# A two-level product scheme on one core: gated factors and modulation steps given out by an account of VectorE's work, weight sums moved from GpSimd to VectorE, raw weights fetched one pair ahead

## The chip, the cores and the metric

One core of one Trainium2 chip runs the whole program. The metric is the device time in microseconds, the median of several runs. The profile is one further execution, recorded by the hardware profiler.

## What is computed

One layer of a diffusion backbone over 1024 latent tokens and 256 context tokens, D_MODEL 1024, float32 in and out. The two feed-forward parts are what matters here (the second over the latent tokens alone):

```python
def ffn_sublayer(h, shift, scale, gate, g, w_in, w_out):
    hn = modulate(rmsnorm(h, g), shift, scale)
    a, b = jnp.split(hn @ w_in, 2, axis=-1)        # 2 x 2816 columns
    y = (jax.nn.silu(a) * b) @ w_out
    return h + 0.5 * gate[:, None, :] * y

mods = jnp.split(jax.nn.silu(c) @ w_ada[layer] + b_ada[layer], N_MOD, axis=-1)   # 9 vectors of 1024
```

Between the two stand a combined projection, an mLSTM scan, a spatial gating branch and a merge; a final RMSNorm ends it.

## The kernel before, in words

**Products.** Every float32 operand is split into a high and a low part (`split`: ScalarE rounds to fp32r, VectorE subtracts), and each product of 128-wide tiles is three matmuls (high-high, high-low, low-high). Above that the latent products use a scheme with seven block products in place of eight, the numbers 1 to 7 in the code. Their operands are sums and differences of quarter blocks of the weights and of the activations, and their results are added up in PSUM banks and SBUF tiles.

**The gate stages.** `Stage.gate` runs twice, for `w1i` (here gate A, 203 to 639 us in the profile) and for `w2i` (gate B, 2081 to 2512 us). `Gate` goes through 22 column tiles f of the feed-forward width (11 pairs f, f + 11), seven steps each, 12 matmuls of 512 columns per step. The first three tiles are the head: they run in step-major order (`HSEQ`) while the activation factors (`Factors.late`) are still being made. The others run tile by tile in the order `SEQ` = 1, 6, 5, 7, 2, 4, 3. Steps 1 and 2 share a bank, as do 6, 7 and 4, and 5 and 3. After 6, 7, 4 and 3 VectorE reads the bank (u at L396, y at L399 and L400, p at L405 and L406, u at L409 and L411), and the bank's next product must wait for that read.

**Weights.** `Gate.load` takes the next (f, p) of the order, forms the weight factor and splits it into a page of the ring. Steps 1, 2 and 4 use a raw quarter as it is; 5, 6, 7 and 3 need sums (`presum`: two operations on GpSimd, L342 and L343; one more for 6, L358, and one for 3, L360). The raw half pages (512 KB, `half`) lie in four pages, two for each tile. `fill` keeps 4 weights ready, and 4 + `ring2` (7) from the first step 3 on, where the pages of the activations' h are given back and a second pool opens. The head's raw pages and presums come earlier, in `preload`.

**Gated factors.** When both tiles of a pair are done, `Gate.out` queues ten small pieces of work: four subtractions on VectorE and six stores, three of which split first (tile `fhl`). They lie in `todo`, a queue that every product serves: after each three matmuls of 512 columns `pump(512)` adds credit, and when there are 512 units the next piece is issued and its cost taken off. Pieces are taken strictly in order.

**Modulation.** `tick` moves a generator (`ada_steps`) on by one: it loads a 128 x 512 piece of `w_ada` (tile `adapg`, two pages) and adds it, scaled, to two sums on VectorE (L735, L737); every ninth step transposes and reduces them. In gate A it is called directly after every fourth step, once the second pool is open; the output stage that follows calls it too.

**Order on the engines.** What is described here is the order in which instructions are issued to the tile context. When that context closes, it plans the order of the instructions on each engine, with what is issued earlier preferred among what is ready, gives out the pages and inserts the waits. SP issues all DMAs named here, from one queue.

Of the kernel before, what the change touches and what calls it, by code (L numbers as in the profile page):

```python
# [13 lines left out]
ALU = mybir.AluOpType  # L14
# [40 lines left out]


def _build(ctx, tc, nc, a, out):
    V, S, G, T = nc.vector, nc.scalar, nc.gpsimd, nc.tensor

# [37 lines left out]
    def t2(name, dt=F32, shape=(128, 512)):  # L97
        return tp.tile(list(shape), dt, name=name, tag="t2", bufs=12)

    def mm_ps(name):  # L100
        return ps.tile([128, 512], F32, name=name, tag="mm", bufs=4)

    def sm_ps(name):
        return ps.tile([128, 512], F32, name=name, tag="sm", bufs=4)

    class Weights:
# [9 lines left out]
        def load(self):  # L116
            n, i, w = self.order.popleft()
            src = a[n][i]
            raw = self.pool.tile([128, w], F32, name="raw", tag="raw", bufs=2)
            nc.sync.dma_start(raw, src)  # L120
            hl = self.pool.tile([128, 2, w], F32R, name="hl", tag="hl", bufs=3)
            split(hl, raw)
            self.ready.append((n, i, hl))
            self.held += 1
# [8 lines left out]
        def done(self, n=1):  # L133
            self.held -= n
            while self.order and self.held < 3:
                self.load()

    def split(hl, src):
        S.copy(hl[:, 0, :], src)  # L139
        V.tensor_sub(hl[:, 1, :], src, hl[:, 0, :].bitcast(F32))  # L140

    todo = deque()
# [4 lines left out]
    credit = [0]  # L147

    def pump(w):
        credit[0] = min(credit[0] + w, 512) if todo else 0  # L150
        while todo and credit[0] >= 512:
            f = todo.popleft()
            credit[0] -= COST(f)
            f()

    def flush():
        while todo:
            todo.popleft()()
# [153 lines left out]
    class Gate:  # L312
# [14 lines left out]
        def fill(self):  # L327
            while self.order and self.held < self.depth:
                self.load()

        def half(self, f, i):
            s = self.s.setdefault(f, {})
            if i not in s:
                s[i] = self.raw(f)
                nc.sync.dma_start(s[i], a[self.name][2 * f + i])
            return s[i][:, 0:512], s[i][:, 512:1024]

        def presum(self, f):
            a1, a2 = self.half(f, 0)
            b1, b2 = self.half(f, 1)  # L340
            s1 = self.s[f]["s1"] = self.sums("s1")
            G.tensor_tensor(s1, b1, b2, ALU.add)  # L342
            G.tensor_tensor(b1, a1, b1, ALU.subtract)  # L343

        def load(self):
            f, p = key = self.order.popleft()
            if p in (1, 2):
                src = self.half(f, 0)[p - 1]
                self.half(f, 1)
            else:  # L350
                a1, a2 = self.half(f, 0)
                b1, b2 = self.half(f, 1)
                s = self.s[f]

                if p in (5, 6) and "s1" not in s:
                    self.presum(f)
                if p == 6:
                    G.tensor_tensor(a1, s["s1"], a1, ALU.subtract)  # L358
                elif p == 3:
                    G.tensor_tensor(a2, a2, a1, ALU.subtract)  # L360
                src = {6: a1, 5: s["s1"], 7: b1, 4: b2, 3: a2}[p]
            hl = self.ring()
            split(hl, src)
            self.ready.append((key, hl))
            self.held += 1
            if p == 3:
                del self.s[f]

        def prod(self, pt, f, p, pages, first):
            key, hl = self.ready.popleft()  # L370
# [12 lines left out]
        def step(self, f, p, pages, store):  # L383
            u = self.u.setdefault(f, {})
            bank = {1: "A", 2: "A", 6: "B", 7: "B", 4: "B", 5: "C", 3: "C"}[p]
            first = p in (1, 6, 5)
            if first:
                u[bank] = mm_ps("qa") if bank == "A" or bank == "B" and f in self.head else sm_ps("qb")
            pt = u[bank]
            self.prod(pt, f, p, pages, first)  # L390
            if p == 1:
                u["p1"] = t2("p1")
                S.copy(u["p1"], pt)
            elif p == 6:
                u["u1"] = t2("u1")
                V.tensor_add(u["u1"], u["p1"], pt)  # L396
            elif p == 7:
                u["y2"] = t2("y2")
                V.tensor_add(u["y2"], u["p1"], pt)  # L399
                V.tensor_add(u["y2"], u["y2"], u["C"])  # L400
            elif p == 2:
                u["x1"] = t2("x1")
                S.activation(u["x1"], pt, AF.Silu)
            elif p == 4:
                V.tensor_add(u["p1"], u["p1"], pt)  # L405
                V.tensor_mul(u["x1"], u["x1"], u["p1"])  # L406
            elif p == 3:
                x2 = u["u1"]
                V.tensor_add(x2, x2, pt)  # L409
                S.activation(x2, x2, AF.Silu)  # L410
                V.tensor_mul(x2, x2, u["y2"])  # L411
                self.out(f, u["x1"], x2, store)
                del self.u[f]

        def out(self, f, lo, hi, store):
            kp = f % self.pairs
            if f < self.pairs:
                self.g[kp] = lo, hi
                store(1, kp, lo)
                return  # L420
            lo1, hi1 = self.g.pop(kp)
            mid = t2("ft")

            def sub(d, x, y):
                return lambda: V.tensor_tensor(d, x, y, ALU.subtract)

            def st(p, t):
                return lambda: store(p, kp, t)

            for fn in (st(2, lo), sub(lo1, hi1, lo1), st(5, lo1), sub(mid, hi, lo1), sub(hi1, hi, hi1), st(7, hi1),  # L430
                       st(6, mid), sub(lo, lo, mid), st(4, lo), st(3, hi)):
                fn.cost = 1152
                todo.append(fn)

    OSEQ = (1, 2, 4, 7, 6, 5, 3)
# [99 lines left out]
    def xpage(tag, name, shape=(128, 1024), dt=F32):  # L535
        if not xps:
            xps.append(pool("x"))
        return xps[0].tile(list(shape), dt, name=name, tag=tag, bufs=4)
# [7 lines left out]
    class Stage:  # L546
# [18 lines left out]
        def preload(self):  # L565
            if self.heads:
                f, i = self.heads.pop(0)
                self.q.half(f, i)
                if i:
                    self.q.presum(f)  # L570

        def rpage(self, name, shape=(128, 2, 512), dt=F32R):
            return self.rg.tile(list(shape), dt, name=name, tag="ring2", bufs=self.ring2)
# [16 lines left out]
        def gate(self, items, tick=None):  # L590
            self.fsp = {p: dr.tile([NFP, 128, 512], F32, name=f"fsp{self.nm}{p}") for p in SEQ if p not in HLP}
            self.hlsp = {p: dr.tile([NFP, 128, 2, 512], F32, name=f"fsp{self.nm}{p}") for p in HLP}
            q, F = self.q, self.F
            q.raw = lambda f: xpage("raw", "rawq")
            q.fill()
            todo.extend(items)
            for n, (f, p) in enumerate(q.steps):
                while not F.ready(p):
                    todo.popleft()()
                if p == 3 and self.rg is None:  # L600
                    self.ch.close()
                    self.rg = self.c.enter_context(tc.tile_pool(name="rg" + self.nm, bufs=1, side="right", reuse_waits="tile"))
                    self.n = 0
                    q.depth = 4 + self.ring2
                    q.sums = lambda n: self.rg.tile([128, 512], F32, name=n, tag="sums", bufs=2)
                q.step(f, p, F.pages, self.store)
                if tick is not None and self.rg is not None and n % 4 == 0:
                    tick()
            flush()

        def rawpage(self, f):
# [115 lines left out]
        return pgt  # L727

    def ada_acc(eng, acc, pgt, q, k, first):
        if eng is G:  # L730
            G.tensor_scalar(acc if first else pgt, pgt, sc2[:, q, k:k + 1], 0.0, ALU.mult, ALU.add)
            if not first:
                G.tensor_tensor(acc, acc, pgt, ALU.add)
        elif first:
            eng.tensor_scalar(acc, pgt, sc2[:, q, k:k + 1], 0.0, ALU.mult, ALU.add)  # L735
        else:
            eng.scalar_tensor_tensor(acc, pgt, sc2[:, q, k:k + 1], acc, ALU.mult, ALU.add)  # L737
# [85 lines left out]
    def it(f, *args):  # L823
        return lambda: f(*args)
# [116 lines left out]
    def tick():  # L941
        next(bg, None)
# [62 lines left out]
    for f in range(NF):  # L1005
        hl, g = wready.popleft()
# [362 lines left out]
    for n in range(3):  # L1369
        w = 256 if n == 2 else 512  # L1370
# [474 lines left out]
    def ahead(i):  # L1845
        if i == 0:
            heads[0].coeff(0)
            heads[0].coeff(1)
            heads[0].inter()
        elif i == 6:  # L1850
            heads[0].kq()
        elif i == 7:
            for k in range(4):
                for tb in range(2):
                    load_split(yb, ybsp, tb, k)
# [208 lines left out]
```

## Time and profile before

| | |
|---|---|
| median of 3 runs | 2746.61 us (2743.4 to 2750.3) |
| the profiled execution: span from first to last instruction | 2740.7 us; its own time is not given apart from the span |
| busy, of the span | TensorE 97%, VectorE 71%, ScalarE 39%, GpSimd 21% |
| granted TensorE clock, mean | 0.994 |
| gate A | 202.7 to 638.7 us |
| gate B | 2080.6 to 2512.1 us |

In the profile PE is TensorE's matmuls, PEld its weight loads, DVE VectorE, ACT ScalarE, POOL GpSimd, SP the queue that issues DMAs. A row of the timeline begins with start and duration in us; what stands in brackets at its end is how long the engine had been idle and whose work ended that. "x12" is a count of merged instructions. `out<-in` are the tiles by the program's names. In a row of waits the three numbers are the total, the number of waits and the longest.

### The profile page before, as it was taken

The numbers are of one execution on the slowest core, as the hardware profiler recorded it, in microseconds if no ns is written. First come the engines' busy times: TensorE is split into PE (matmuls) and PEld (weight loads), VectorE is DVE, ScalarE is ACT, GpSimd is POOL, SyncE is SP. The second block draws the span as 40 slices with busy tenths as digits, with TensorE's granted clock in tenths as the row PEclk, the third lists the DMA queues.
The fourth block names the chain that finished last, engine by engine and source line by source line (L and its number), as shares of the span: only waits on it lengthen the run. The fifth ranks groups of instructions, "written<-read, shape, count | busy, mean of one in ns | idle before, by whom it ended". The sixth has DMA issues, their size and how long they took to land.

```text
span 2740.7 us, 35737 instructions
## 1 busy us (share of the span) xinstructions
PE 2665.6 (97%) x12734; PEld 2212.6 (81%) x12734; DVE 1957.4 (71%) x3305; ACT 1082.5 (39%) x1862; POOL 576.8 (21%) x518
## 2 busy tenths in 40 slices
PE   8899999999999999999999999999999999999998
PEld 4787788788888878877888888888877788888887
DVE  4787887777968746667665678768478866666755
ACT  3563333334436625444434333112245333333432
POOL 0102333220000121232221315443011323230000
PEclk9999999999999999999999999999999999999999
DMA  8851443439668421227554357547341333336645
GB/s 285 276 192 66 167 149 132 146 123 316 223 210 274 142 93 65 93 100 240 175 169 150 108 185 263 194 158 265 116 138 54 127 127 112 131 123 243 210 156 171
DMA packets 199585, 456.74 MB, mean 167 GB/s; under 512 B 20592, under 2 KB 49008, under 8 KB 199408
## 3 DMA queue, kind: packets, MB, share of 16 engines
q1 hardware_dynamic: 199408, 454.47, 48.7%
q8 instruction: 100, 1.64, 0.2%
q14 instruction: 77, 0.63, 0.1%
HBM read 328.95 MB, written 125.51 MB: 166 GB/s over the span
## 4 chain that ended last, share of the span: by engine, by line
PE 49%; DVE 5%; issue 4%; POOL 1%; DMA 1%; ACT 1%; SPq 0%; POOLq 0%; DVEq 0%; ACTq 0%
PE pq L1221 12%; PE qb L376 9%; PE pt L1689 8%; PE po L495 6%; PE qa L376 4%; PE pr L1140 3%; PE pn L1802 2%; PE pu L1529 2%; DVE ring L140 1%; PE pn L1800 1%; PE pkc L1201 1%; DMA adapg<-in_w_ada_dram 1%; POOL rawq L1186 1%; DVE adacc L737 1%; POOL rawq L1187 1%
## 5 line engine op out<-in xcount | busy, mean ns | idle before, releaser
L139 ACT CAST ring<-rawq 128x512 fp32r<-128x512 f32 x432 | 266.4, 620 | 589.7 <-PE qb L376 147.6
L140 DVE TENSOR_TENSOR ring<-rawq,ring 128x512 fp32r<-128x512 f32 x432 | 331.9, 770 | 197.0 <-ACT ring L139 194.8
L495 PE MATMUL po<-gring,wring 128*128 128x512 f32 (+1 forms) x1896 | 424.9, 385 | 0.3 <-DMA gring<-fsp 0.3
L495 PEld LDWEIGHTS po<-gring,wring 128*128 128x128 f32 x1896 | 349.6, 188 | 71.5 <-issue 1.4
L376 PE MATMUL qb<-fc,ring 128*128 128x512 f32 x1440 | 345.7, 394 | 16.1 <-DVE u L396 8.6
L376 PEld LDWEIGHTS qb<-fc,ring 128*128 128x128 f32 x1440 | 272.9, 190 | 76.9 <-DVE y L399 9.8
L376 PE MATMUL qa<-fa,ring 128*128 128x512 f32 x1056 | 253.4, 390 | 0.5 <-ACT ring L139 0.5
L376 PEld LDWEIGHTS qa<-fa,ring 128*128 128x128 f32 x1056 | 197.9, 188 | 42.7 <-ACT ring L139 0.9
L1221 PE MATMUL pq<-fc,ring 128*128 128x512 f32 x864 | 216.8, 400 | 14.4 <-ACT py L1232 9.7
L376 PE MATMUL qb<-fb,ring 128*128 128x512 f32 x984 | 229.5, 389 | 0.0
L376 PEld LDWEIGHTS qb<-fb,ring 128*128 128x128 f32 x984 | 184.7, 188 | 38.4
L1221 PEld LDWEIGHTS pq<-fc,ring 128*128 128x128 f32 x864 | 162.3, 190 | 52.9 <-ACT py L1232 11.6
L139 ACT CAST wring<-rw 128x512 fp32r<-128x512 f32 x154 | 95.7, 622 | 230.3 <-PE po L495 192.3
L1689 PE MATMUL pt<-yp,ring 128*128 128x512 f32 x768 | 184.3, 396 | 0.0
L140 DVE TENSOR_TENSOR wring<-rw,wring 128x512 fp32r<-128x512 f32 x154 | 106.0, 688 | 94.0 <-ACT wring L139 93.8
L1689 PEld LDWEIGHTS pt<-yp,ring 128*128 128x128 f32 x768 | 144.1, 188 | 29.3
L1221 PE MATMUL pq<-fa,ring 128*128 128x512 f32 x576 | 141.0, 392 | 0.2 <-ACT px L1227 0.2
L1221 PE MATMUL pq<-fb,ring 128*128 128x512 f32 x576 | 137.8, 393 | 0.0
L737 DVE SCALAR_TENSOR_TENSOR adacc<-adapg,sc,adacc 128x512 f32<-128x512 f32 x140 | 120.1, 871 | 16.5 <-DMA adapg<-in_w_ada_dram 14.9
L1221 PEld LDWEIGHTS pq<-fb,ring 128*128 128x128 f32 x576 | 107.8, 188 | 22.9 <-PE pu L1570 0.4
L1221 PEld LDWEIGHTS pq<-fa,ring 128*128 128x128 f32 x576 | 107.0, 188 | 23.7 <-ACT px L1227 1.3
L139 ACT CAST ring<-rawt 128x512 fp32r<-128x512 f32 x64 | 39.6, 619 | 185.1 <-PE pt L1689 173.1
(341 smaller groups left out, 4424.7 us busy)
## 6 DMA issues: line engine op xcount, KB each, us to landing
adapg<-in_w_ada_dram SPq DMA_DIRECT2D x144, 256.0 KB, 3.9
fsp<-fhl SPq DMA_DIRECT2D x66, 512.0 KB, 2.9
gring<-fsp SPq DMA_DIRECT2D x66, 512.0 KB, 3.6
raw<-in_w1i_dram SPq DMA_DIRECT2D x44, 512.0 KB, 4.8
graw<-fsp SPq DMA_DIRECT2D x88, 256.0 KB, 3.6
rawq<-in_w1i_dram SPq DMA_DIRECT2D x38, 512.0 KB, 3.9
rawq<-in_w2i_dram SPq DMA_DIRECT2D x38, 512.0 KB, 3.3
fsp<-x SPq DMA_DIRECT2D x66, 256.0 KB, 2.1
```

What stands on the lines that cost most here:

```text
L139: S.copy(hl[:, 0, :], src)
L140: V.tensor_sub(hl[:, 1, :], src, hl[:, 0, :].bitcast(F32))
L376: T.matmul(pt, hl[:, x, sl], pages[p][k][:, y, :], start=first and i == 0, stop=i == 11, skip_group_check=not first)
L495: T.matmul(pt[:, cs], w[:, x, sl], g[:, y, cs], start=grp and kp == 0 and i == 0, stop=kp == NFP - 1 and i == 2, skip_group_check=not grp)
L737: eng.scalar_tensor_tensor(acc, pgt, sc2[:, q, k:k + 1], acc, ALU.mult, ALU.add)
L1140: T.matmul(self.pt[m], pg[:, x, sl], hl[:, y, :], start=first and k == 0 and i == 0, stop=k == 3 and i == 2, skip_group_check=not first)
L1186: G.tensor_tensor(b2, b2, b1, ALU.subtract)
L1187: G.tensor_tensor(a1, a1, b2, ALU.add)
L1221: T.matmul(pt, hl[:, x, k * 128:(k + 1) * 128], pg[k][:, y, :], start=first and k == 0 and i == 0, stop=k == 3 and i == 2, skip_group_chec ...
L1529: T.matmul(pu[:, 0:257], ksl[:, kt * 128:(kt + 1) * 128], wv, start=True, stop=True)
L1689: T.matmul(pt, hl[:, x, k * 128:(k + 1) * 128], pg[:, y, :], start=kh + k + i == 0, stop=kh == 1 and k == 3 and i == 2)
L1802: T.matmul(pn[:, 0:257], qi[:, c_, :], self.C[d][:, c_, :], start=False, stop=c_ == 1)
```

## The change

Four things, all around the gate stages:

- A number `debt` accounts for VectorE's issued work: `dv(w)` adds 62 + 0.77 w units for an operation over w columns, `pump(w)` takes w off (not below 0). Splits, the reads of the banks, the weight sums, the subtractions of the gated factors and the modulation's additions are charged.
- The ten pieces of `Gate.out` cost 640 units instead of 1152 and are marked `later`; a `later` piece at the head of `todo` is issued only when `debt` is under 128. The modulation step of every fourth gate step is no longer called directly but queued in `todo` in the same way. In the output stage `tick` is called as before.
- The weight sums of `Gate.load` and its `presum` go to VectorE. Only the head's presums, in `preload`, stay on GpSimd.
- `ahead` issues the raw loads of the next two tiles not yet loaded, once before the first step and then whenever a tile's last weight has been formed. The number of raw pages stays four.

```diff
+    debt = [0.0]
+
+    def dv(w=512):
+        debt[0] += 62 + 0.77 * w
+
     def split(hl, src):
+        dv(hl.shape[-1])
         S.copy(hl[:, 0, :], src)
         V.tensor_sub(hl[:, 1, :], src, hl[:, 0, :].bitcast(F32))
...
     def pump(w):
         credit[0] = min(credit[0] + w, 512) if todo else 0
-        while todo and credit[0] >= 512:
+        debt[0] = max(debt[0] - w, 0.0)
+        while todo and credit[0] >= 512 and (debt[0] < 128 or not getattr(todo[0], "later", False)):
             f = todo.popleft()
...
+        def ahead(self):
+
+            for f in list(dict.fromkeys(f for f, _ in self.order if f not in self.head))[:2]:
+                for i in range(2):
+                    self.half(f, i)
+
...
-        def presum(self, f):
+        def presum(self, f, eng):
             a1, a2 = self.half(f, 0)
             b1, b2 = self.half(f, 1)
             s1 = self.s[f]["s1"] = self.sums("s1")
-            G.tensor_tensor(s1, b1, b2, ALU.add)
-            G.tensor_tensor(b1, a1, b1, ALU.subtract)
+            if eng is V:
+                dv()
+                dv()
+            eng.tensor_tensor(s1, b1, b2, ALU.add)
+            eng.tensor_tensor(b1, a1, b1, ALU.subtract)
...
                 if p in (5, 6) and "s1" not in s:
-                    self.presum(f)
+                    self.presum(f, V)
                 if p == 6:
-                    G.tensor_tensor(a1, s["s1"], a1, ALU.subtract)
+                    dv()
+                    V.tensor_tensor(a1, s["s1"], a1, ALU.subtract)
                 elif p == 3:
-                    G.tensor_tensor(a2, a2, a1, ALU.subtract)
+                    dv()
+                    V.tensor_tensor(a2, a2, a1, ALU.subtract)
...
             if p == 3:
                 del self.s[f]
+                if f not in self.head:
+                    self.ahead()
...
             def sub(d, x, y):
-                return lambda: V.tensor_tensor(d, x, y, ALU.subtract)
+                def run():
+                    dv()
+                    V.tensor_tensor(d, x, y, ALU.subtract)
+                return run
...
-                fn.cost = 1152
+                fn.cost, fn.later = 640, True
                 todo.append(fn)
...
             q.fill()
+            q.ahead()
             todo.extend(items)
...
                 if tick is not None and self.rg is not None and n % 4 == 0:
-                    tick()
+                    fn = it(tick)
+                    fn.cost, fn.later = 640, True
+                    todo.append(fn)
...
     def ada_acc(eng, acc, pgt, q, k, first):
+        dv()
```

The rest of the diff charges `dv()` where `Gate.step` reads a bank (512 columns after 6, 1024 after 7, 4 and 3) and passes GpSimd to `presum` in `preload`.

More of the change, by code (lines that the diff above doesn't have):

```diff
@@ L397, in step @@
             elif p == 7:
+                dv(1024)
                 u["y2"] = t2("y2")
@@ L404, in step @@
             elif p == 4:
+                dv(1024)
                 V.tensor_add(u["p1"], u["p1"], pt)
@@ L407, in step @@
             elif p == 3:
+                dv(1024)
                 x2 = u["u1"]
@@ L569, in preload @@
                 if i:
-                    self.q.presum(f)
+                    self.q.presum(f, G)
         def rpage(self, name, shape=(128, 2, 512), dt=F32R):
@@ L729, in ada_acc @@
     def ada_acc(eng, acc, pgt, q, k, first):
+        dv()
         if eng is G:
```

## The prediction

> **What bounds the kernel now.** I read the page first, then the waits of TensorE in the two gate stages, then TensorE's timeline there, then VectorE and GpSimd side by side. The page's first two lines and one row of the windows for each gate:
>
> ```profile
> span 2740.7 us, 35737 instructions
> PE 2665.6 (97%) x12734; PEld 2212.6 (81%) x12734; DVE 1957.4 (71%) x3305; ACT 1082.5 (39%) x1862; POOL 576.8 (21%) x518
> 202.70:638.70 436.00, 425.13 (x1853) 348.70 (x1854) 345.32 (x482) 155.45 (x266) 124.92 (x82) 0.99 0.41 140
> 2080.60:2512.10 431.50, 424.14 (x1860) 349.23 (x1859) 311.24 (x438) 166.00 (x286) 117.88 (x80) 0.99 0.33 120
> ```
>
> TensorE is busy for 97% of the span, so no edit away from it can pay more than the time in which it stands still. In the gates (columns: length, then busy time and count of PE, PEld, DVE, ACT, POOL, clock, DMA share, GB/s) VectorE is busy for 79% (345.32 of 436.00) and 72%. The waits, first of gate A, then of gate B:
>
> ```profile
> PE qb L376 <- DVE y L399: 7.5, 4, 4.2
> PE qb L376 <- DVE u L396: 3.3, 3, 2.0
> PE qb L376 <- DVE u L396: 5.3, 1, 5.3
> ```
>
> So TensorE waits 10.8 us in gate A and 5.3 us in gate B for VectorE to read a bank of sums (u after p 6, y after p 7), which must be done before the next product adds to that bank, one product later. Where they fall:
>
> ```profile
> 270.59 3.02 PE L376 MATMUL qb<-fc,ring 128*128 128x512 f32 x12 [2.01 <-DVE u L396]
> 280.55 8.62 PE L376 MATMUL qb<-fc,ring 128*128 128x512 f32 x24 [4.22 <-DVE y L399]
> 291.73 5.60 PE L376 MATMUL qb<-fb,ring 128*128 128x512 f32 x24
> 2156.34 4.97 PE L376 MATMUL qb<-fc,ring 128*128 128x512 f32 x12 [5.30 <-DVE u L396]
> 255.00:285.00 30.00, 23.77 (x95) 18.80 (x95) 28.77 (x38) 10.65 (x19) 12.22 (x8) 0.91 0.43 148
> 2136.00:2156.00 20.00, 15.05 (x67) 12.13 (x65) 17.27 (x24) 7.76 (x14) 8.82 (x6) 0.94 0.30 100
> ```
>
> Two places hold most of it: the end of the head in each gate, where the ring grows from 4 to 7 pages, so that four weights are prepared at once. There the clock in the windows falls to 0.91 and 0.94, and the matmuls after the long waits run slow: 8.62 us where 24 take 5.60 (3.0 us lost), and 4.97 where 12 take half of 5.60 (2.2 us lost). So the end of the head costs 2.0 + 4.2 + 3.0 = 9.2 us in A and 5.3 + 2.2 = 7.5 us in B. The other 4.6 us of A (10.8 less 6.2) are short waits elsewhere. Together 21.3 us, 0.8% of the run.
>
> **Weight sums by VectorE instead of GpSimd.** First the timeline of gate B, GpSimd and VectorE side by side; then groups: four of gate A (255 to 639 us), the last two of gate B (2100 to 2512). A group's columns are its count, busy time, mean ns of one, and the idle time before it with its releaser.
>
> ```profile
> 2304.59 1.63 POOL L343 TENSOR_TENSOR rawq<-rawq 128x512 f32<-128x512 f32 x1
> 2302.83 0.69 DVE L409 TENSOR_TENSOR u<-u,qb 128x512 f32<-128x512 f32 x1 [0.73 <-PE qb L376]
> 2304.98 1.78 DVE L411 TENSOR_TENSOR u<-u,y 128x512 f32<-128x512 f32 x1
> ```
>
> ```profile
> L140 DVE TENSOR_TENSOR ring<-rawq,ring 128x512 fp32r<-128x512 f32 x113 | 87.8, 777 | 23.5 <-ACT ring L139 22.6
> L140 DVE TENSOR_TENSOR ring<-s,ring 128x512 fp32r<-128x512 f32 x19 | 19.0, 1001 | 2.4 <-ACT ring L139 2.3
> L425 DVE TENSOR_TENSOR ft<-u,x 128x512 f32<-128x512 f32 x10 | 15.6, 1556 | 0.0
> L140 DVE TENSOR_TENSOR fhl<-u,fhl 128x512 fp32r<-128x512 f32 x10 | 6.8, 683 | 0.0
> L411 DVE TENSOR_TENSOR u<-u,y 128x512 f32<-128x512 f32 x21 | 30.8, 1466 | 0.0
> L140 DVE TENSOR_TENSOR ring<-rawq,ring 128x512 fp32r<-128x512 f32 x114 | 87.6, 770 | 47.3 <-ACT ring L139 46.7
> ```
>
> An addition on VectorE takes 0.68 to 0.69 us (fhl: 683 ns), but 1.78 us when a sum of GpSimd runs beside it: L411 at 2304.98 ends at 2306.76, just after GpSimd's L343 (2306.22). L409, which reads a PSUM bank, keeps its 0.69. Over gate A this stretch is 113 x 0.09 + 19 x 0.31 + 10 x 0.87 = 25 us in three groups; over gate B 21 x 0.78 + 114 x 0.08 = 25 us in two. It goes with the sums. Added: all 82 sums that gate A's window has on GpSimd (80 in B's; the first two sums of each head weight are issued earlier and stay on GpSimd). Back to back one costs 0.61 us, as 2143.14 and 2143.75 below stand apart, so 50 us in each gate. Net VectorE is 25 us busier in each gate: 370 of 436 us (85%) in A and 335 of 431 (78%) in B. That lies beside TensorE as long as no bank is read late, so on average it costs nothing; the cover is the product between p 6 and p 7, 2.8 us (half of the 5.60 of 24 matmuls), or four operations of VectorE. What counts is the two crowded places, where this cover is gone already.
>
> (The Trainium skill, "Perfetto Trace Analysis", Optimizing Scalar/DVE Operations, speaks against the move: with VectorE full, work may go to GpSimd, though between those two it "might not help", since they share a read port. By its first half the move loads a full engine, which is the second rival below; by its second half nothing is won or lost, which is the first. The rows show an engine that is full in places only.)
>
> **The end of the head, gate A.**
>
> ```profile
> 252.91 3.07 DVE L140 TENSOR_TENSOR ring<-rawq,ring 128x512 fp32r<-128x512 f32 x2
> 255.90 1.77 DVE L406 TENSOR_TENSOR x<-x,p 128x512 f32<-128x512 f32 x1
> 271.76 1.29 DVE L140 TENSOR_TENSOR ring<-rawq,ring 128x512 fp32r<-128x512 f32 x2 [1.22 <-ACT ring L139]
> 273.57 1.78 DVE L425 TENSOR_TENSOR x<-x,ft 128x512 f32<-128x512 f32 x1
> 276.48 1.75 DVE L140 TENSOR_TENSOR ring<-s,ring 128x512 fp32r<-128x512 f32 x1
> 278.15 1.75 DVE L737 SCALAR_TENSOR_TENSOR adacc<-adapg,sc,adacc 128x512 f32<-128x512 f32 x1
> ```
>
> Between 252 and 281 us the pair lost 1.8 us (3.07 against 1.29), the four others 1.0 to 1.1 each, the wait 1.2: 7.2 us. The eight sums of the window add 8 x 0.61 = 4.9. Net VectorE is 2.3 us earlier. The second relief is the account (next part): it holds back the gated factors (four subtractions and three splits) and the first modulation step, up to 4 us of which stood ahead of the late reads. Relief between 2.3 and 6.3 us, against 6.2 us of waiting; I take 4.7, nearer the upper end because the account is charged for just this crowd. That leaves a wait of 1.5, and after the wait of 2.01 us at 270.59 the twelve matmuls took 3.02 us, not slow. Gain 4.7 + 3.0 = 7.7, with ends 2.3 and 9.2.
>
> **The end of the head, gate B.**
>
> ```profile
> 2136.58 1.78 DVE L406 TENSOR_TENSOR x<-x,p 128x512 f32<-128x512 f32 x1
> 2142.49 0.62 ACT L139 CAST ring<-rawq 128x512 fp32r<-128x512 f32 x1 [6.58 <-POOL rawq L358]
> 2143.14 0.69 DVE L140 TENSOR_TENSOR ring<-rawq,ring 128x512 fp32r<-128x512 f32 x1 [2.49 <-ACT ring L139]
> 2143.75 0.69 DVE L411 TENSOR_TENSOR u<-u,y 128x512 f32<-128x512 f32 x1
> 2145.55 0.68 DVE L425 TENSOR_TENSOR x<-u,x 128x512 f32<-128x512 f32 x1
> 2151.93 1.63 DVE L425 TENSOR_TENSOR x<-x,ft 128x512 f32<-128x512 f32 x1
> 2155.52 0.68 DVE L396 TENSOR_TENSOR u<-p,qb 128x512 f32<-128x512 f32 x1
> ```
>
> The chain is GpSimd, ScalarE, VectorE: ScalarE has stood 6.58 us for GpSimd's sum, and VectorE 2.49 us for ScalarE's copy. With the sums on VectorE that wait shrinks to about one copy (0.62 and the way there), 1.7 us less; three stretched operations, from 2136.58 to 2151.93, give back 1.1, 1.1 and 0.9 us; the window's six sums add 3.7. Net 1.1 us. The gated factors of the first pair (from 2145.55 on: some six operations, 3.7 us) stand ahead of u at 2155.52 and are held back. Relief 1.1 to 4.8 against a wait of 5.3; I take 3.8, for the same reason as in A. A wait of 1.5 is left and the 2.2 us of slow matmuls goes: gain 6.0, ends 1.1 and 7.5.
>
> **The account and the steps' order.** A step of four pumps drains 2048 units in some 2.8 us, and an operation is charged 62 + 0.77 x 512 = 456, which is 0.62 us: the scale fits the rows. One pair of factors (14 steps, 28,672 units) is charged 14 splits, 14 operations that read banks, 8 sums and 7 operations of gated factors, 43 in all, or 67%; in gate A 3.5 modulation steps add two each, 78%. So the queue keeps up, and nothing piles up for the stage's end. Following the rule through the head, the first gated factor is issued at step 22.75 instead of 20.25 (7 us later); in the later pairs it comes one step after the pair is born. But issue is not position: the context plans each engine's order itself. A modulation step is issued every four steps (11 us), yet the loads stand in groups, with a gap of 72 us between these two (SP), and so do VectorE's modulation operations:
>
> ```profile
> 393.11 0.33 SPq L726 DMA_DIRECT2D adapg<-in_w_ada_dram  x1
> 465.34 2.23 SPq L726 DMA_DIRECT2D adapg<-in_w_ada_dram  x2
> 597.00:624.00 27.00, 26.39 (x117) 21.33 (x116) 25.77 (x40) 9.37 (x16) 4.45 (x3) 1.00 0.50 165
> ```
>
> In such a group VectorE is full (25.77 of 27.00 us) and the 4.6 us of short waits of gate A stand there. The sums make these groups fuller, the missing stretch makes them emptier; the account hardly moves what the context pulls forward. I put them at 0, ends a gain of 4.6 and a loss of 5.5 (three such groups, three sums in each as in the row, at 0.61 with no stretch returned).
>
> **Raw weights one pair ahead.** On SP, gate A:
>
> ```profile
> SPq L335 <- DVE ring L140: 132.6, 34, 12.0
> POOL s L342 <- DMA rawq<-in_w1i_dram: 1.7, 2, 1.3
> ```
>
> All 34 raw loads already wait 3.9 us each for a page that VectorE must give back, and only two sums waited for a load. With four pages an earlier issue cannot start them earlier. What queues behind them on SP are the stores of factors and the adapg loads, which wait there today too. Cost 0, ends -1.7 and +1.7.
>
> **Sum.** 7.7 + 6.0 + 0 + 0 = 13.7 us: span 2740.7 to 2727.0. The median of the runs, 2746.6, stands 5.9 us above the profiled span; with the same distance the time is 2732.9.
>
> **The rivals.** *No change that can be measured* (0.3%, 8.2 us, is what a measurement tells here). The net of stretch and sums alone pays 2.3 + 1.1 us, and if the context plans the factors where they stood, only that and the slow matmuls of one gate (3.0) come: 6.4 us, 2740.2. For it: the modulation loads stand where the planner wants them. Against it: the factors read results that exist only after the head's last products. Chance 0.27.
>
> *Slower: VectorE's sums land in the crowd.* If the stretch came from something else than GpSimd's sums, the 8 + 6 sums of the two places and the 9 in the groups of A, 23 x 0.61 = 14.0 us, all stand ahead of a bank's read where there is no slack: 2760.6; with half of it covered, 2753.6. It decides from the point where returned stretch and held-back factors fall below 4.9 us in A's place and 3.7 us in B's. Against it: every 1.7 to 1.8 us row quoted has a sum beside it. For it: net VectorE time does rise. Chance 0.16.
>
> *All waits go*: 21.3 us, 2725.3; a part of the forecast's case, which ends there.
>
> **How the numbers follow.** The forecast's case, waits at the ends of the head mostly gone, has 0.57, from 2725 to 2738; that is also "faster". "Same" is the first rival, 0.27; "slower" the second, 0.16. The range runs from 2724, a microsecond below all waits gone, to 2754, the second rival with half its price covered.
>
> **What would show it.** Right: GpSimd nearly empty between 203 and 640 and between 2080 and 2512 us; VectorE's L411 and ring splits at 0.69 us; no wait over 2 us at L376 near 270 to 281 and near 2151, no clock of 0.91 there; VectorE busy near 85% in gate A. Wrong: new waits of TensorE for u or y inside the modulation groups, VectorE operations above 1 us with GpSimd idle, VectorE waiting for adapg loads that are now issued in bunches, or raw loads that start earlier than a page's release.

## The result and the profile after

| | before | after |
|---|---|---|
| median of 4 runs each, one chip | 2745.01 us | 2722.64 us (2719.57 to 2723.34) |
| ratio | | 0.9912, 95% interval 0.9900 to 0.9924 |
| profiled span | 2740.7 us | 2720.4 us |
| gate A, first matmul to the output stage's first | 435.95 us | 422.29 us |
| between the two gates | 1441.94 us | 1444.25 us |
| gate B | 431.44 us | 422.87 us |

The change makes the kernel 22.4 us faster, more than forecast. The two gates give 13.7 and 8.6 us; the rest of the program is the same within 2.3 us. The page of the changed kernel, and the windows that answer to those of before (gate A, gate B, the ends of the two heads; length, then busy time and count of PE, PEld, DVE, ACT, POOL, clock, DMA share, GB/s):

```profile
span 2720.4 us, 35602 instructions
PE 2661.8 (98%) x12734; PEld 2210.9 (81%) x12734; DVE 1974.2 (73%) x3469; ACT 1085.2 (40%) x1862; POOL 330.0 (12%) x354
202.00:624.40 422.40, 421.19 (x1853) 346.93 (x1854) 350.55 (x563) 156.58 (x267) 0.00 (x0) 1.00 0.43 144
2068.50:2491.50 423.00, 421.47 (x1861) 347.87 (x1860) 324.81 (x517) 167.06 (x286) 0.00 (x0) 1.00 0.34 123
254.30:284.30 30.00, 30.00 (x134) 24.82 (x133) 29.91 (x51) 13.87 (x25) 0.00 (x0) 1.00 0.50 174
2123.60:2143.60 20.00, 20.00 (x90) 16.56 (x89) 19.95 (x34) 9.21 (x17) 0.00 (x0) 1.00 0.31 108
```

GpSimd does nothing in the gates. At the ends of the heads TensorE is busy without a break at full clock, where it had 23.77 of 30 and 15.05 of 20 us, although VectorE is now as good as full there (29.91 of 30.00, 19.95 of 20.00). VectorE has about 80 operations more in each gate and is busier by only 5.2 us in A (345.32 to 350.55) and 13.6 us in B (311.24 to 324.81). What is left of TensorE's waits for VectorE's reads in the products of the gates (qa and qb; the rows are from the view of the whole program):

```profile
PE qa L396 <- DVE u L417: 1.5, 1, 1.5
PE qb L396 <- DVE u L417: 0.8, 2, 0.6
PE qb L396 <- DVE y L421: 0.4, 1, 0.4
```

The same groups as before, gate A (the splits of the ring, the sum of step 6 in its new place, ft), then L435 (L411 before) in gate B; and a stretch of VectorE's timeline at the end of A's head:

```profile
L146 DVE TENSOR_TENSOR ring<-rawq,ring 128x512 fp32r<-128x512 f32 x113 | 77.7, 688 | 15.2 <-ACT ring L145 14.8
L146 DVE TENSOR_TENSOR ring<-s,ring 128x512 fp32r<-128x512 f32 x19 | 13.0, 686 | 1.6 <-ACT ring L145 1.5
L375 DVE TENSOR_TENSOR rawq<-s,rawq 128x512 f32<-128x512 f32 x19 | 13.1, 689 | 0.3
L451 DVE TENSOR_TENSOR ft<-u,x 128x512 f32<-128x512 f32 x10 | 6.8, 684 | 0.0
L435 DVE TENSOR_TENSOR u<-u,y 128x512 f32<-128x512 f32 x21 | 14.4, 684 | 0.0
```

```profile
259.54 0.68 DVE L451 TENSOR_TENSOR x<-u,x 128x512 f32<-128x512 f32 x1
262.54 0.68 DVE L146 TENSOR_TENSOR fhl<-x,fhl 128x512 fp32r<-128x512 f32 x1
264.35 0.69 DVE L451 TENSOR_TENSOR u<-u,u 128x512 f32<-128x512 f32 x1
265.55 0.68 DVE L417 TENSOR_TENSOR u<-p,qb 128x512 f32<-128x512 f32 x1
266.15 0.48 DVE L766 TENSOR_SCALAR adacc<-adapg,sc 128x512 f32<-128x512 f32 x1
271.98 0.68 DVE L421 TENSOR_TENSOR y<-p,qb 128x512 f32<-128x512 f32 x1
```

Two things are to be seen. First, no group is stretched: 688 for 777 ns, 686 for 1001, 684 for 1556, 684 for 1466. Second, three of the five operations of the gated factors that stood ahead of u (L451 and fhl here) still stand ahead of it, although the account issues them later. The modulation's operations do stand behind it now (L766 at 266.15). Run 1 finds u and y as early without the account, so what brought them forward (to 265.55 and 271.98, from 269.86 and 279.82) is left to the experiments.

### The profile page after: what moved, and what is told of

Read it like the earlier page. It is cut to its first block, busy times and chain, and to the rows that moved or that the text cites. A ratio compares the mean times of both kernels' runs of the same rounds, so it can differ in the third digit from the quotient of the medians.

```text
span 2720.4 us, 35602 instructions
## 1 busy us (share of the span) xinstructions
PE 2661.8 (98%) x12734; PEld 2210.9 (81%) x12734; DVE 1974.2 (73%) x3469; ACT 1085.2 (40%) x1862; POOL 330.0 (12%) x354
## 4 chain that ended last, share of the span: by engine, by line
PE 52%; DVE 5%; issue 2%; POOL 1%; DMA 1%; ACT 1%; SPq 0%; POOLq 0%; DVEq 0%; ACTq 0%
PE pq L1252 13%; PE qb L396 10%; PE pt L1720 9%; PE po L522 6%; PE qa L396 5%; PE pr L1171 3%; PE pn L1833 2%; PE pu L1560 2%; PE pn L1831 1%; DVE ring L146 1%; PE pkc L1232 1%; DMA adapg<-in_w_ada_dram 1%; PE pm L1677 1%; POOL rawq L1217 0%; POOL rawq L1218 0%
## 5 line engine op out<-in xcount | busy, mean ns | idle before, releaser
L146 DVE TENSOR_TENSOR ring<-rawq,ring 128x512 fp32r<-128x512 f32 x432 | 311.1, 722 | 185.9 <-ACT ring L145 183.6
L396 PE MATMUL qb<-fc,ring 128*128 128x512 f32 x1440 | 340.0, 390 | 1.1 <-DVE u L417 0.8
L768 DVE SCALAR_TENSOR_TENSOR adacc<-adapg,sc,adacc 128x512 f32<-128x512 f32 x140 | 110.6, 803 | 14.4 <-DMA adapg<-in_w_ada_dram 13.5
```

Source lines behind the costliest of these rows:

```text
L396: T.matmul(pt, hl[:, x, sl], pages[p][k][:, y, :], start=first and i == 0, stop=i == 11, skip_group_check=not first)
```

## The experiments

Two theories stood after the result. **S**: GpSimd's sums stretched VectorE's operations (an operation lasts longer beside a sum), and that alone made TensorE wait. **A**: what stood ahead of the bank reads made them late, and the account clears it. Runs 1 to 4, runs 5 to 7 with the first of 9, and run 8 with the last two of 9 were taken on three chips, each group beside its own runs of the kernel before, whose median is given with each; times of different groups are compared by their ratios.

**1. The sums alone.**

```diff
 # the kernel before, in Gate.load (presum likewise: G -> V, in preload still G)
-                    G.tensor_tensor(a1, s["s1"], a1, ALU.subtract)
+                    V.tensor_tensor(a1, s["s1"], a1, ALU.subtract)
...
-                    G.tensor_tensor(a2, a2, a1, ALU.subtract)
+                    V.tensor_tensor(a2, a2, a1, ALU.subtract)
```

> The kernel before with one part of the change: the 82 weight sums of each gate on VectorE, nothing else (modulation steps and gated factors given out as before, no earlier fetch). Theory S (GpSimd's sums stretched VectorE's operations, and that alone made TensorE wait): nearly the whole gain of the changed kernel, 17 to 22 us below before, no VectorE operation of 512 columns above 0.8 us in the gates, waits of L376 under 3 us in all. Theory A (what stood ahead of the bank reads made them late, and only the account clears it): 3 to 8 us below before, the waits at the ends of the two heads still 1 to 4 us each.

Measured 2725.39 us beside 2747.79: ratio 0.9921 (0.9905 to 0.9937). That is the whole gain. The windows of its two gates and the one kind of wait for a bank's read in gate A:

```profile
203.80:626.20 422.40, 421.09 (x1852) 347.03 (x1853) 350.40 (x563) 156.57 (x266) 0.00 (x0) 1.00 0.43 144
2073.30:2496.30 423.00, 421.48 (x1859) 347.79 (x1858) 324.96 (x517) 167.16 (x286) 0.00 (x0) 1.00 0.34 123
PE qb L376 <- DVE u L396: 1.3, 3, 0.6
```

**2. The account alone.** The changed kernel with the sums back on GpSimd and uncharged, and without `ahead`.

```diff
-                    self.presum(f, V)
+                    self.presum(f, G)
...
-                    dv()
-                    V.tensor_tensor(a1, s["s1"], a1, ALU.subtract)
+                    G.tensor_tensor(a1, s["s1"], a1, ALU.subtract)
```

> The other half: the account gives out gated factors and modulation steps, but the sums stay on GpSimd (and are not charged), no earlier fetch. Theory S: within 5 us of before, VectorE operations of 1.7 us as before, waits of TensorE at the ends of the heads 8 us or more in all. Theory A: 10 to 18 us below before.

Measured 2747.66 us beside 2747.79: ratio 0.9997 (0.9988 to 1.0006), no change. TensorE's waits, gate A and then gate B, are spread otherwise and cost the same; the gates take 435.3 and 430.6 us:

```profile
PE qb L392 <- DVE y L417: 6.9, 4, 2.6
PE qb L392 <- DVE u L413: 2.4, 2, 2.0
PE qb L392 <- DVE y L417: 3.6, 1, 3.6
```

**3. The change without the earlier fetch.**

```diff
             q.fill()
-            q.ahead()
...
-                if f not in self.head:
-                    self.ahead()
```

> The changed kernel without the earlier fetch of raw weights. If the fetch is worth nothing, since the four pages hold every load back until VectorE gives one up: the changed kernel's time within 2 us. Rival (the fetch removes waits for loads): 3 us or more above the changed kernel, with VectorE's sums waiting for raw loads for more than the 6.6 us that they wait in the changed kernel's gate A.

Measured 2726.07 us beside 2747.79: ratio 0.9919 (0.9907 to 0.9932), the changed kernel's within the interval. On SP the raw loads of gate A wait for VectorE with the fetch as they do without it. With it (the changed kernel):

```profile
SPq L348 <- DVE ring L146: 111.7, 33, 11.5
DVE s L358 <- DMA rawq<-in_w1i_dram: 6.6, 7, 1.8
```

In run 3 the first of these rows reads 111.5 us in 32 waits; in the kernel before it is 132.6 us in 34. VectorE's sums wait no longer for their loads without the fetch either: 4.1 us against 6.6.

**4. The stretch again.** The change, with four idle additions on GpSimd for every tile.

```diff
                 if p == 6:
                     dv()
                     V.tensor_tensor(a1, s["s1"], a1, ALU.subtract)
+                    G.tensor_tensor(junk, s["s1"], a1, ALU.add)
```

and likewise one after step 3's sum and two after `presum`.

> The whole change, and GpSimd does four idle additions of the same size for every tile beside VectorE's own (their results are used by nothing). VectorE then has its own sums and is stretched again. Theory S: VectorE is some 40 us a gate busier and TensorE waits for bank reads; the time comes back to before or goes above it, 2740 to 2765. Theory A (order decides, stretch is covered): within 6 us of the changed kernel.

Measured 2761.15 us beside 2747.79: ratio 1.0044 (1.0032 to 1.0056), the only slower kernel of all. The window of gate A and TensorE's waits there:

```profile
204.00:651.00 447.00, 428.55 (x1853) 347.54 (x1854) 397.39 (x562) 154.16 (x266) 113.89 (x82) 0.99 0.39 135
PE qb L402 <- DVE u L423: 12.0, 10, 1.9
PE qb L402 <- DVE y L427: 6.0, 5, 4.0
```

VectorE has the work of the changed kernel (x562) and is busy for 397 us instead of 351. No wait of TensorE, VectorE or SP in this gate is put down to GpSimd, and the gate is 447.1 us long instead of 422.3. Gate B takes 431.2 us (422.9).

**5. The change once more**, beside the next three.

> The changed kernel as it is, beside the next three. 2722 to 2726 us. With the sums alone at 2725.4 and the change without the fetch at 2726.1, theory S0 (account and fetch are worth nothing once the sums are on VectorE) puts it within 2 us of both; a rival, that account and fetch together bring a few more us, at 2721 or less.

Measured 2719.93 us beside 2741.56: ratio 0.9924 (0.9912 to 0.9937). The time itself lies below the 2722 to 2726 us that were expected and in the rival's range, but on this chip the kernel before is 6.2 us faster as well. Against a ratio of 0.9921 for the sums alone, account and fetch have no part that can be measured.

**6. The idle additions on VectorE.** As 4, with `V.tensor_tensor(junk, ...)`.

> The change, with the four idle additions of each tile on VectorE instead of GpSimd: no stretch, but VectorE has 82 x 0.61 = 50 us more in each gate, 400 of 422 us in A (95%) and 375 of 423 in B (89%). Theory C (VectorE's load as such binds from about nine tenths): gate A 10 to 30 us longer, gate B nearly unchanged. Theory S (a stretched operation costs more than one of its own): below the 2761 us with the idle additions on GpSimd. Rival (load is covered up to 100%): within 4 us of the changed kernel.

Measured 2724.95 us beside 2741.56: ratio 0.9934 (0.9921 to 0.9946). That is 5.0 us above run 5, more than the 4 us of the rival that the load is covered, but with overlapping intervals. Its two gates:

```profile
202.00:624.00 422.00, 421.47 (x1856) 347.29 (x1855) 390.00 (x640) 155.50 (x265) 0.00 (x0) 1.00 0.42 143
2068.00:2492.00 424.00, 422.35 (x1863) 348.54 (x1862) 370.96 (x598) 166.16 (x286) 0.00 (x0) 1.00 0.34 123
```

With 640 operations instead of 563 VectorE is busy for 390 of 422 us (92%), and gate A is no longer (421.55 us; gate B takes 423.2). Theory C falls: load as such does not bind up to there. An addition on GpSimd that nothing needs costs more than the same one on VectorE: 447.1 against 421.6 us.

**7. No sums.** This kernel is the one before, but leaves out the lines of the sums and splits the raw weights in their place.

```diff
-                if p in (5, 6) and "s1" not in s:
-                    self.presum(f)
-                if p == 6:
-                    G.tensor_tensor(a1, s["s1"], a1, ALU.subtract)
-                elif p == 3:
-                    G.tensor_tensor(a2, a2, a1, ALU.subtract)
-                src = {6: a1, 5: s["s1"], 7: b1, 4: b2, 3: a2}[p]
+                src = {6: a1, 5: s.get("s1", b2), 7: b1, 4: b2, 3: a2}[p]
```

> The kernel before without the weight sums after the head's first presums: the weights of products 5, 6, 7 and 3 are split raw, so that part of the computation is left out. Neither GpSimd nor VectorE has them. Theory S: the gates are free of waits and the time is that of the changed kernel within 3 us, for moving the sums already removed all that they cost. Rival (VectorE's 82 additions a gate still cost something beside TensorE): 4 to 10 us below the changed kernel.

Measured 2716.86 us beside 2741.56: ratio 0.9909 (0.9894 to 0.9924), 3.1 us below the change (run 5), with overlapping intervals. That lies between theory S (within 3 us) and its rival (4 us or more): moving the sums removed nearly all that they cost, and a small cost of VectorE's additions is not excluded. Its gates take 419.8 and 422.2 us, where run 5 has 421.7 and 422.9:

```profile
202.00:621.50 419.50, 419.50 (x1853) 347.04 (x1852) 304.07 (x482) 156.53 (x266) 0.00 (x0) 1.00 0.43 146
2064.00:2486.00 422.00, 421.46 (x1859) 347.68 (x1858) 282.30 (x438) 166.90 (x286) 0.00 (x0) 1.00 0.34 123
```

This measures the stretch: VectorE's 482 and 438 operations are those of the kernel before, which took 345.32 and 311.24 us. GpSimd's sums cost VectorE 41 us in gate A and 29 in gate B. On VectorE itself the sums take 46.5 and 42.5 us (the changed kernel's 350.55 and 324.81 less 304.07 and 282.30).

**8. GpSimd in the chain without reading.** A rival was still open: the chain itself, in which ScalarE's rounding waits for GpSimd's sum and VectorE's subtraction for ScalarE. Here GpSimd's sums are memsets of the same tiles.

```diff
-                    G.tensor_tensor(a1, s["s1"], a1, ALU.subtract)
+                    fill_(a1, 3)          # G.memset(a1, 0.0), three times
```

> The kernel before with GpSimd's weight sums replaced by GpSimd memsets of the same tiles, two or three in a row for each sum, so that GpSimd stays in the chain of every weight for about as long (1.0 to 1.6 us) but reads nothing from SBUF. The values of the weights of products 5, 6, 7 and 3 are thus left out. Theory S (the stretch cost the time): VectorE's operations keep 0.69 us, the gates are 419 to 423 us long as in the run without sums, 20 us or more below before. Rival L (the time went to the chain GpSimd, ScalarE, VectorE at the ends of the heads): waits of 3 us or more return there, 5 to 15 us above the run without sums.

Measured 2723.52 us beside 2747.26: ratio 0.9915 (0.9902 to 0.9929). Gate A takes 421.1 us, gate B 422.8, where the kernel without sums has 419.8 and 422.2; no wait at the ends of the heads is above 0.6 us. Gate A (the window, GpSimd's memsets, the ring's splits):

```profile
203.00:623.00 420.00, 419.07 (x1856) 345.88 (x1855) 303.93 (x482) 157.65 (x269) 105.32 (x205) 1.00 0.43 144
L357 POOL MEMSET rawq<- 128x512 f32 x146 | 75.6, 534 | 217.0 <-DVE ring L140 203.7 <-DMA rawq<-in_w1i_dram 10.0
L357 POOL MEMSET s<- 128x512 f32 x37 | 19.4, 527 | 75.8 <-DVE fc L140 37.8 <-DVE ring L140 37.1
L140 DVE TENSOR_TENSOR ring<-rawq,ring 128x512 fp32r<-128x512 f32 x114 | 78.3, 689 | 33.5 <-ACT ring L139 32.4
```

GpSimd is busy for 105 us of the gate and in the chain of every weight that has a sum, and VectorE is as busy as without sums (303.93 us). At the end of gate A's head the 22 operations of the kernel before stand ahead of u, and they take 13.5 us instead of 17.0. The rival falls: in the gates the time went to GpSimd's reading of SBUF. (The Trainium skill, "SBUF — State Buffer", Who interferes with whom, says just this: a VectorE instruction with two SBUF inputs contends with a GpSimd instruction that reads SBUF, not with one that only writes. The rows agree: 689 ns beside memsets, 1.78 us beside sums, and 0.69 for the one that reads PSUM.) One kind of operation is lengthened beside memsets too: TENSOR_SCALAR, with one tensor and a column of scalars as inputs. The four of L206 at the start of gate B take 1.43 us in all, against 0.87 without sums and 1.88 beside a sum.

**9. All sums on VectorE.** Between the gates the projection's weights have the same sums (`Rows`, `Pair`).

```diff
 # in Rows.load and Pair.load, eight places
-                G.tensor_tensor(b1, a1, b1, ALU.subtract)
+                V.tensor_tensor(b1, a1, b1, ALU.subtract)
```

> The change, and the sums of the projection's weights between the gates (8 places in Rows and Pair, 120 operations on GpSimd) go to VectorE as well. There VectorE is busy for six to seven tenths and TensorE waits some 14 us for it and for ScalarE after products 7 and 5 (py). Theory S: VectorE's stretched operations there go too, 4 to 10 us below the changed kernel. Rival (those waits have another cause, the order of bank reads on ScalarE, and VectorE is not late there): within 3 us.

Measured 2699.47 us beside 2741.56: ratio 0.9845 (0.9832 to 0.9859), 20 us below the change and twice the upper end of what was expected (the pages count 128 sums moved, not 120); the time between the gates went from 1442.3 us (run 5) to 1423.0. From 900 to 1480 us, the changed kernel first, then this one:

```profile
900.00:1480.00 580.00, 563.80 (x2587) 460.86 (x2587) 370.21 (x567) 255.20 (x448) 148.24 (x106) 0.99 0.40 132
900.00:1480.00 580.00, 577.91 (x2681) 475.54 (x2681) 410.17 (x692) 266.51 (x464) 3.65 (x6) 1.00 0.40 134
```

In the same stretch TensorE does 94 matmuls more. TensorE's waits for ScalarE after product 7 are gone too, of which the changed kernel's page of waits has

```profile
PE pq L1252 <- ACT py L1263: 9.3, 5, 2.1
```

The profile puts them down to ScalarE, which has the same 1862 instructions in both programs; moving GpSimd's sums ended them. Which way is not shown. In this stretch the changed kernel has VectorE's splits stretched (763 ns against 691), but ScalarE also waits 67.6 us for GpSimd's sums, and only 32.7 us for VectorE's once they are there. Memsets were tried in the gates alone.

Its two companions: the same without account and fetch, and the same again.

> The kernel before with the sums of the gates and of the projection's weights on VectorE, without account and without fetch. Theory S0 (account and fetch are worth nothing): the time of the change with all sums moved (2699 beside a before of 2741.6, ratio 0.9845) within 3 us. Rival (the account matters once VectorE is fuller): 5 us or more above it.

> The change with all sums moved once more, beside the kernel without account and fetch: ratio 0.984 to 0.986 to the kernel before.

Measured 2703.86 and 2703.04 us beside 2747.26: ratios 0.9840 (0.9827 to 0.9854) and 0.9841 (0.9827 to 0.9854). So the kernel before with all these sums written for VectorE is as fast as any here; account and fetch add nothing to it that can be measured.

## Why the prediction was wrong

The mechanism was there and the place too: GpSimd's sums stretched VectorE's operations, and TensorE waited for that at the ends of the heads. Terms of the sum were too small, and one part was credited to the wrong edit.

- *The step that failed: the relief at the ends of the heads, "Net VectorE is 2.3 us earlier" (1.1 in gate B), raised with the account to 4.7 and 3.8, so that a wait of 1.5 us was left in each.* It takes the sums' own time (4.9 and 3.7 us) off the returned stretch, as though every sum made the line of work ahead of the late reads longer. Measured, nothing of these waits was left. The table follows VectorE at the end of gate A's head; the line of work runs from the first split of a raw weight (252.91 us before) to the read of u.

| | operations ahead of u | they take, us | u read after the gate's first matmul, us | y read, us |
|---|---|---|---|---|
| before | 22 | 17.0 | 67.1 | 77.1 |
| account alone (run 2) | 22 | 17.0 | 67.1 | 77.1 |
| the change | 21 | 12.8 | 63.5 | 69.9 |
| sums alone (run 1) | 22 | 13.0 | 63.6 | 70.3 |
| no sums (run 7) | 22 | 13.0 | 63.2 | 68.8 |
| memsets (run 8) | 22 | 13.5 | 63.6 | 69.3 |

In the change five sums stand ahead of u, but two operations of the gated factors and four of the modulation stand behind it instead; run 1, without the account, has four sums there and four of the others behind. So the line got no longer there, and the stretch came back in full. In gate B the change has 21 operations for 22, in 12.8 us for 19.5, of which 2.5 were the wait for ScalarE; run 1 has 26 there and still takes 15.8. In run 2 the same 22 operations stand in the same order as before: the account moved nothing here. The prediction also missed one stretched row, L735 below (1.51 us for 0.48); with it, 3.9 us of stretch stand ahead of u. Four rows of the kernel before:

```profile
257.60 1.51 DVE L735 TENSOR_SCALAR adacc<-adapg,sc 128x512 f32<-128x512 f32 x1
269.86 0.68 DVE L396 TENSOR_TENSOR u<-p,qb 128x512 f32<-128x512 f32 x1
279.82 0.68 DVE L399 TENSOR_TENSOR y<-p,qb 128x512 f32<-128x512 f32 x1
2086.00 1.88 DVE L206 TENSOR_SCALAR diag<-cst,rs_y 128x128 f32<-128x128 f32 x4
```

- *"I take 4.7 ... because the account is charged for just this crowd."* Wrong, and against the prediction's own next paragraph, which says that issue is not position. The modulation loads had shown it.
- *The modulation groups at 0.* The second term that was too small: gate A is 13.7 us shorter, and the end of its head accounts for 9.2. Of the short waits, 4.6 us, 1.2 are left, and TensorE's busy time fell by 3.9 us where 3.0 were counted for slow matmuls. The end named for this, a gain of 4.6, was right.
- *A wait that was not listed.* Gate B is 8.6 us shorter, 1.1 more than the 7.5 at its head. At its start L206 (last row above) took 1.88 us beside a sum of GpSimd and takes 0.88 now, and TensorE's wait of 1.1 us for it is gone.
- *"Over gate A this stretch is ... 25 us ... over gate B ... 25 us", and so "Net VectorE is 25 us busier in each gate".* Too small in A: by run 7 the stretch was 41 and 29 us, and VectorE became busier by 5.2 and 13.6. This did not enter the time, but it made the move look dearer than it was. The sum was made over three groups of A and two of B. Four of the groups of A that went uncounted, from the kernel before (202.7 to 638.7 us):

```profile
L737 DVE SCALAR_TENSOR_TENSOR adacc<-adapg,sc,adacc 128x512 f32<-128x512 f32 x56 | 46.8, 853 | 1.3 <-DMA adapg<-in_w_ada_dram 1.2
L140 DVE TENSOR_TENSOR ring<-rawh,ring 128x512 fp32r<-128x512 f32 x18 | 15.5, 872 | 6.7 <-ACT ring L139 6.7
L735 DVE TENSOR_SCALAR adacc<-adapg,sc 128x512 f32<-128x512 f32 x8 | 6.8, 869 | 0.0
L140 DVE TENSOR_TENSOR fc<-h,fc 128x512 fp32r<-128x512 f32 x10 | 8.3, 827 | 2.6 <-ACT fc L139 2.2
```

Against the undisturbed 746, 688, 481 and 688 ns these are 6.0 + 3.3 + 3.1 + 1.4 = 14 us, and smaller groups make up the 41. The whole price was to be had from one view.
- *VectorE's load covered by TensorE.* Right, and by far: 92% in gate A (run 6) does not lengthen gate A. As an argument for a small gain it should have had no weight.
- *The fetch at 0.* Right (run 3).
- *The slower rival.* Its condition did not hold. Run 4 made one like it, and 14.0 us forecast stand beside 13.4 measured, but that is partly luck: gate A grew by 11 us, in waits spread over the whole stage, and gate B not at all (431.2 us).
- *The median, "5.9 us above the profiled span".* Every run on record whose span is listed lies 1.7 to 2.1 us above its own span, so most of the 5.9 was the choice of the execution that was profiled; after the change the median stands 2.2 us above the span. The difference is 3.7 of the 10.3 us by which the time came below the forecast. The other 6.6 are 8.5 that the gates gave beyond 13.7, less 1.9 that the rest of the program lost.
- *The range.* "All waits go" was priced 2725.3 and the lower end put a microsecond below. Nearly all went, and the unlisted wait of gate B with them: the case itself had been given too little.

Of the marks named, these came true: GpSimd empty, operations at 0.69 us, no wait near 270, 281 and 2151, no clock of 0.91; VectorE's share in gate A is 83% (85 forecast).

## What to carry to other kernels

Before moving element-wise work between VectorE and GpSimd, sum what VectorE's operations last above their undisturbed duration, over all groups, while GpSimd reads SBUF beside them; that is part of the price of GpSimd's share and appears under other lines. Here additions with one input from PSUM were not lengthened, and GpSimd instructions that only write did not lengthen additions. Nor may the moved operations simply be added to the line of work ahead of a late read: the planner may put others behind it. And where a planner orders the engines, an edit to the order of issue is to be checked in the order that comes out, before it is credited with anything.

## What the runs showed of the hardware

Gate A's sums, some 80 additions that take 46.5 us on VectorE, raised VectorE's busy time there by only 5.2 us when taken from GpSimd. As many idle additions on VectorE raised it by 39 us (run 6, 77 more operations in its window); done by GpSimd they raised it by 47 us (run 4). VectorE at 92% with bank reads due within one product of 2.8 us did not lengthen gate A. TENSOR_SCALAR on VectorE was lengthened by GpSimd's sums (869 ns in the mean, 481 undisturbed) and, where it ran beside one, by a memset too (L206 in run 8, 1.43 us for four against 0.87).
